# The overflow branch of an expert layer moved ahead of the first expert, and a hold on the last gate's weight splits

## The chip, the cores and the metric

The kernel runs on one core of one Trainium2 chip. The metric is the device time of one execution in microseconds, median of three runs. All times below are us unless marked ns.

## The reference

Two decoder layers over 256 tokens of width 1024, in float32. Layer 0 has a dilated attention, a dense feed-forward and a gated embedding; layer 1 has a sliding-window attention with sinks, an expert layer (the two best of 8 experts per token) and a gated embedding; a last norm ends it. The change is in the expert layer of layer 1 and in the gated product behind it:

```
logits = (h @ w_router); top_v, top_i = lax.top_k(logits, 2); wts = softmax(top_v)
gates  = einsum(one_hot(top_i, 8), wts)
for e in range(8):
    y = y + gates[..., e:e+1] * ((silu(h @ w1[e]) * (h @ w3[e])) @ w2[e])   # 1024 -> 3584 -> 1024
x = x + y
gate = sigmoid(rmsnorm(x) @ ple_w_gate);  x = x + (p @ ple_w_proj) * gate
return rmsnorm(x)
```

The weights of the 8 experts are 352 MB, 336 blocks of 1 MiB; each is read once.

## The kernel before

**Experts.** The experts are ranked by their number of tokens. Rank r has a fixed number of slots, `CAPS` (96 for the first five, 64 for the last three), and the ranks are computed in the order `TURNS = (0, 5, 1, 2, 6, 3, 4, 7)`. Rank 0 stands in the code as expert 0 itself; which expert the others are is known only at run time. Tokens that find no slot are computed by `beyond` (line 1448), a block of instructions under `tc.If(most > 0)` (line 1466); `most` is the largest overflow, read into a register of every engine by `values_load` (line 1441). In the runs here no token is left over, so the branch jumps over the block. It stands between the fourth and the fifth expert: `by_turn(TURNS[:4], ...)` (line 1438) and `by_turn(TURNS[4:], ...)` (line 1511) are two sequences, and each ends with its last sum and combine exposed. The false side of the branch holds one semaphore instruction on PE, ACT and DVE and eight on SP, one for each of the semaphores that count SP's transfers. Each waits until its semaphore has the value of everything issued so far, and then adds what the skipped block would have added.

**One expert.** `Expert` (line 1140) makes a selection matrix `P` from token positions (DVE), `gather` multiplies it with the normed tokens (32 PE products, two ACT copies to `xb`) and turns `P` into `PT`. Four chunks of the hidden width follow (1024, 1024, 1024, 512). `hidden` (line 1217) forms `H` from `w1` and `w3` in 32-column groups of PE; `hidden_tail` does silu (ACT), the product (DVE), the turning to `hT` (PE, ACT or DVE); `output` (line 1265) sums `w2` products into `Y`, one chunk behind `hidden`. After the last chunk `combine` (line 1176) copies and splits `Y` into `yh`, `yl` (ACT, DVE), spreads them back with `PT` (8 PE products) and adds to `x` (DVE). Within a sequence, gather and combine of neighbours are laid between the chunks' products.

**Routing.** `route` (line 1343) is a generator: counts of tokens by products with triangular and one matrices, `Expert` for rank 0 and its gather, then on DVE the ranking (it ends in `cnt`, ranks and overflow as integers), then the gate values (lines 1391 to 1403, DVE and one ACT exponential). `find` (line 1423) loads the seven expert numbers into registers of SP.

**Weights.** `Stream` (line 152) lists all weight blocks in order of use. SP issues them in that order, each as soon as its buffer's last reader is done; the expert layer has 17 buffers (5 `raw`, 2 `mwa`, 10 `mwb`; the `mwb` are given up after `ple_w_proj`, in the last expert's third chunk). So 17 blocks can be issued before the first expert starts. The blocks of `ple_w_gate` come last; `Stream.piece` (line 266) splits each in four pieces into a rounded part `whi` (ACT, with the norm's gain) and the rest `wlo` (DVE), in one of three buffers.

**Order.** The order on each engine's queue is fixed when the program is written, by a planner (`Flow`, line 49). It keeps a clock `now`, a time at which each engine's queue ends, and a time at which each tile is due (a block of weights 2.70 after the one before it, plus 0.95; an ACT pass over 512 columns 0.52; a split's pass on DVE 0.66; a group of four products of 512 columns 0.85). Generators are run when their time comes. The generator `Stream.ahead` (line 298) appends a piece of a split when the queues of ACT and DVE end less than `slack` (2.5 in this stage) after `now`; it is started by `next_raw` (line 253) whenever blocks to be split are loaded.

Of the kernel before, what the change touches and what calls it, by code (L numbers as in the profile page):

```python
# [15 lines left out]
OP = mybir.AluOpType  # L16
AX = mybir.AxisListType
PSUM = bass.MemoryType.PSUM

D = 1024  # L20
S = 256
NB = 2
# [6 lines left out]
NE = 8  # L29
# [122 lines left out]
class Stream:  # L152
# [3 lines left out]
    def __init__(self, nc, act, vec, flow, rawp, look, width, nraw=NRAW):  # L156
        self.nc = nc
        self.act = act
        self.vec = vec
        self.flow = flow  # L160
        self.hls = []
        self.look = look
        self.width = width
        self.phase(0)
        self.part = None
        self.specs = []
        self.loaded = 0
        self.conv = 0
        self.used = 0
        self.raw = {}  # L170
        self.ready = {}
        self.times = {}
        self.dma = 3000.0
        self.done = {}
        self.pools = []
        self.more(rawp, nraw, "raw", -1)
# [76 lines left out]
    def next_raw(self, held=0):  # L253

        i = self.used
        self.ahead_raw(i - held)
        self.load(i + 1)
        t, c, n, before, _ = self.raw.pop(i)
        self.landed(t, c * n, before)
        self.used += 1  # L260
        self.skip_raw()
        if self.conv < self.loaded:
            self.flow.start(self.ahead(self.loaded, i - held))
        return t[:, :c * n].rearrange("p (c n) -> p c n", c=c)

# [70 lines left out]
def trunk(ctx, tc, x, p, attn_norm, ffn_norm, a_w_qkv, a_w_o, kv_norm, kv_w, b_w_q, b_sinks,  # L336
# [113 lines left out]
    add_square(st, b_w_o[0])  # L450
    moe0 = len(st.specs)
    ranks = [(r,) if r else 0 for r in TURNS]
    add_moe(st, moe_seq(ranks[:4]))
    moe_cut = add_moe(st, moe_seq(ranks[4:]), 3 * len(moe_chunks) + PLE_AT, rows(ple_w_proj[1], 0, 256, 0, D))
    add_square(st, ple_w_gate[1], gcol[:, 5, :])


# [844 lines left out]
    def experts(es, nxt=None, then={}, ahead=True):  # L1302

        E = {}
        nf = len(moe_chunks)

        def begin(i):
            E[i] = es[i]()
            return E[i].gather()

        def products(i, res, f, Y):
            output(E[i], Y, res, moe_chunks[f][1], f == 0, f == nf - 1)
            if f == nf - 1:
                flow.start(E[i].combine(Y, nxt if i == len(es) - 1 else None))

        prev = None
        for i in range(len(es)):
            if i not in E:
                g = begin(i)
                if not E[i].ready:  # L1320
                    flow.spawn(g)
            Y = [psY.tile([128, 512], F32, name=f"Y{k}", tag=f"Y{k}") for k in (range(3) if E[i].ng == 3 else (0,))]
            for f, (f0, fn) in enumerate(moe_chunks):
                res = []
                g = begin(i + 1) if ahead and f == nf - 2 and i + 1 < len(es) else None
                hidden(E[i], fn, res)
                if (i, f) in then:
                    then[i, f]()
                if not ahead:
                    products(i, res, f, Y)  # L1330
                    continue
                if g is not None:
                    flow.spawn(g)
                if prev is not None:
                    products(*prev)
                prev = (i, res, f, Y)
            if not ahead:
                flow.drain()
        if ahead:
            products(*prev)  # L1340
        flow.drain()

    def route():

        while 0 not in n_f1.chosen:
            yield flow.now + 100.0
        yield flow.due(sel)
        ps = acc()
        mm(ps[:, 0:8], tri, sel[:, 0], start=True, stop=False, skip_group_check=True)
        mm(ps[:, 8:16], ones, sel[:, 0], start=False, stop=False, skip_group_check=True)  # L1350
        mm(ps[:, 16:24], ones, sel[:, 0], start=False, stop=False, skip_group_check=True)
        while 1 not in n_f1.chosen:
            yield flow.now + 100.0
        yield flow.due(sel)
        mm(ps[:, 8:16], tri, sel[:, 1], start=False, stop=False, skip_group_check=True)
        mm(ps[:, 16:24], ones, sel[:, 1], start=False, stop=True, skip_group_check=True)
        vec.scalar_tensor_tensor(posm.rearrange(g16), sel.rearrange(g16), -BIG, ps[:, 0:16], op0=OP.mult, op1=OP.add)
        if WARM2:
            warm(WARM2)
        first.append(Expert(CAPS[0], posm[:, :, 0:1], by_rank[1][:, :, 0:1]))  # L1360
        vec.tensor_copy(count, ps[:, 16:24])
        yield from first[0].gather()

        d8, a8, perm = d4[:, 0], a4[:, 0], d4[:, 1]
        vec.tensor_copy(total, count)
        vec.memset(total[:, 0:1], 2.0 * S)
        vec.tensor_tensor(d8, total[:, None, :].to_broadcast([128, NE, NE]),
                          total[:, :, None].to_broadcast([128, NE, NE]), op=OP.subtract)
        d, a = d8.rearrange(f64), a8.rearrange(f64)
        vec.scalar_tensor_tensor(a, d, 0.0, less, op0=OP.is_equal, op1=OP.mult)  # L1370
        vec.scalar_tensor_tensor(a, d, 0.0, a, op0=OP.is_gt, op1=OP.add)
        vec.tensor_reduce(rstat[:, 0:8], a8, axis=AX.X, op=OP.add)
        vec.tensor_scalar(rstat[:, 0:8], rstat[:, 0:8], -BIG, None, op0=OP.add)

        vec.tensor_tensor(perm, iota[:, 0:8][:, :, None].to_broadcast([128, NE, NE]),
                          rstat[:, None, 0:8].to_broadcast([128, NE, NE]), op=OP.is_equal)
        vec.tensor_tensor(a8, perm, iota[:, None, 0:8].to_broadcast([128, NE, NE]), op=OP.mult)
        vec.tensor_reduce(rstat[:, 0:8], a8, axis=AX.X, op=OP.add)
        vec.tensor_scalar(cnt[:, 0:8], rstat[:, 0:8], BIG, None, op0=OP.add)
        for tb in range(NB):  # L1380
            vec.tensor_tensor(a8, perm, posm[:, tb, None, :].to_broadcast([128, NE, NE]), op=OP.mult)
            vec.tensor_reduce(by_rank[0][:, tb], a8, axis=AX.X, op=OP.add)

        vec.tensor_tensor(a8, perm.rearrange("p r e -> p e r"), capt[:, None, :].to_broadcast([128, NE, NE]), op=OP.mult)
        vec.tensor_reduce(capx, a8, axis=AX.X, op=OP.add)
        vec.tensor_tensor(total, count, capx, op=OP.subtract)
        vec.tensor_reduce(rstat[:, 0:1], total, axis=AX.X, op=OP.max)
        vec.tensor_scalar(cnt[:, 8:9], rstat[:, 0:1], 0.0, None, op0=OP.max)
        ranked.append(True)
        yield flow.now + 1.0  # L1390
        for tb in range(NB):
            vec.tensor_scalar(lg[:, tb], lg[:, tb], n_f1.r[tb], None, op0=OP.mult)
        vec.tensor_reduce(rstat[:, 1:3], lg, axis=AX.X, op=OP.max)
        vec.tensor_tensor(gates, lg, rstat[:, 1:3][:, :, None].to_broadcast([128, NB, NE]), op=OP.subtract)
        act(gates, gates, AF.Exp)
        yield flow.due(gates)
        vec.tensor_tensor(gates, gates, sel, op=OP.mult)
        vec.tensor_reduce(rstat[:, 3:5], gates, axis=AX.X, op=OP.add)
        vec.reciprocal(rstat[:, 5:7], rstat[:, 3:5])
        vec.tensor_tensor(gates, gates, rstat[:, 5:7][:, :, None].to_broadcast([128, NB, NE]), op=OP.mult)  # L1400
        for tb in range(NB):
            vec.tensor_tensor(a8, perm, gates[:, tb, None, :].to_broadcast([128, NE, NE]), op=OP.mult)
            vec.tensor_reduce(by_rank[1][:, tb], a8, axis=AX.X, op=OP.add)
# [7 lines left out]
        psB = pool(f"psS{k}", 2, ps, space=PSUM)  # L1411

    first = []
    ranked = []

    def by_turn(turns, then={}, **kw):

# [4 lines left out]

    def find():

        flow.until(lambda: ranked)
        for r in TURNS:
            if r:
                which[r] = nc.values_load(cnt[0:1, r:r + 1], engines=(mybir.EngineType.SP,), min_val=0, max_val=NE - 1,
# [2 lines left out]
    st.ahead_raw(st.used)  # L1431
    moes = ExitStack()
    flow.start(route())
    flow.until(lambda: first and len(first[0].ready) == 2)
    gst.close()
    banks.close()
    expert_pools(moes, banks, 1)
    by_turn(TURNS[:4], {(0, 0): find})


    most = nc.values_load(cnt[0:1, 8:9], min_val=0, max_val=S,
                          skip_runtime_bounds_check_because="a count of at most 256 tokens")
    st.ahead_raw(st.used)
    main = st
    moes.close()
    banks.close()

    def beyond(i):

# [14 lines left out]
        selp = sel1  # L1464

    with tc.If(most > 0):
        beyond(1)
        with tc.If(most > CAP):
            beyond(2)
    ppp = pool("ppp", 1, side="right")  # L1470
    expert_pools(moes, banks, 3)


    n_p1 = Norm(div=2)
# [18 lines left out]
    def proj_p1():  # L1493
# [13 lines left out]
        st.more_split(pool("hl2", NHL), NHL)  # L1507
        xtpool = pool("xT2", 1)
        st.phase(6)

    by_turn(TURNS[4:], {(3, PLE_AT - 1): load_p1, (3, PLE_AT): proj_p1}, nxt=n_p1.half)
    st.phase(7)
    moes.close()
    banks.close()
# [87 lines left out]
```

## Time and profile before

| what | value |
|---|---|
| median of 3 runs | 1558.57 (1557.28 to 1560.46) |
| the profiled execution, its own time | 1557.69 |
| its span, first to last instruction | 1555.9 |
| PE busy | 1507.0 (97%) |
| DVE, ACT busy | 541.2 (35%), 433.9 (28%) |
| read from HBM | 452.69 MB, mean 292 GB/s |

The profiled execution lies 1.8 over its span and 0.9 under the median. PE counts as busy in almost the whole span, also where products run at half clock, so its share says little; what counts is the rate of its products in each stage, and where its rows have gaps. SP issues four blocks of the expert weights before 600, the next at 616.4 and the last at 1491.7. Lines of the profile are those of the kernel before; line 135 is the helper that records every ACT and DVE operation, so these are told apart by their tiles.

### The profile page before, as it was taken

The numbers are of one execution on the slowest core, as the hardware profiler recorded it, in microseconds if no ns is written. First come the engines' busy times: TensorE is split into PE (matmuls) and PEld (weight loads), VectorE is DVE, ScalarE is ACT, GpSimd is POOL, SyncE is SP. The second block draws the span as 40 slices with busy tenths as digits, with TensorE's granted clock in tenths as the row PEclk, the third lists the DMA queues.
The fourth block names the chain that finished last, engine by engine and source line by source line (L and its number), as shares of the span: only waits on it lengthen the run. The fifth ranks groups of instructions, "written<-read, shape, count | busy, mean of one in ns | idle before, by whom it ended". The sixth has DMA issues, their size and how long they took to land. (4 is left out here: it accounts for less than half of the span.)

```text
span 1555.9 us, 28406 instructions
## 1 busy us (share of the span) xinstructions
PE 1507.0 (97%) x11944; PEld 862.5 (55%) x11944; DVE 541.2 (35%) x1274; ACT 433.9 (28%) x851; POOL 11.3 (1%) x22
## 2 busy tenths in 40 slices
PE   7999999999999999999999999996999999999977
PEld 7999989888888887334333343332343343343325
DVE  6776767654545796200100100202001001201124
ACT  5555555554444775100000000100000010001123
POOL 0000000000000000000000000000000000000000
PEclk9999999999999999999999999997999999999998
DMA  9544445475554442999999999999799999999890
GB/s 280 154 142 143 122 122 170 136 253 186 175 204 162 136 131 78 410 403 408 409 402 408 408 402 409 409 402 382 299 402 408 409 402 409 406 405 408 353 338 28
DMA packets 214583, 455.66 MB, mean 293 GB/s; under 512 B 15440, under 2 KB 97232, under 8 KB 214448
## 3 DMA queue, kind: packets, MB, share of 16 engines
q1 hardware_dynamic: 214128, 453.31, 78.3%
q8 instruction: 95, 1.56, 0.4%
q0 software_dynamic: 176, 0.40, 0.1%
q14 instruction: 40, 0.33, 0.1%
q10 hardware_dynamic: 144, 0.07, 0.0%
HBM read 452.69 MB, written 1.05 MB: 292 GB/s over the span
## 5 line engine op out<-in xcount | busy, mean ns | idle before, releaser
L1137 PE MATMUL H<-mwb,xb 128*32 128x512 f32 (+1 forms) x3176 | 322.9, 540 | 0.2 <-DMA mwb<-in_moe_w 0.2
L135 DVE TENSOR_TENSOR wlo<-raw,whi 128x768 fp32r<-128x768 f32 (+1 forms) x180 | 188.5, 1079 | 117.8 <-ACT whi L135 117.5
L135 DVE TENSOR_TENSOR sa<-sa,H 128x512 f32<-128x512 f32 (+1 forms) x32 | 19.9, 621 | 574.6 <-PE H L1137 574.6
L1137 PEld LDWEIGHTS H<-mwb,xb 128*32 128x32 f32 x3176 | 104.9, 110 | 194.3 <-issue 169.7
L135 ACT ACTIVATE whi<-raw 128x768 fp32r<-128x768 f32 (+1 forms) x180 | 162.0, 945 | 111.0 <-PE scr L347 61.3
L135 ACT ACTIVATE sa<-H 128x512 f32<-128x512 f32 (+1 forms) x32 | 17.4, 544 | 611.0 <-PE H L1137 611.0
L1137 PE MATMUL H<-raw,xb 128*32 128x512 f32 (+1 forms) x1480 | 158.8, 546 | 0.0
L1137 PE MATMUL Y<-mwb,hT 128*32 128x512 f32 x1240 | 143.4, 594 | 0.0
L347 PE MATMUL acc<-whi,xT0h 128*128 128x384 f32 (+2 forms) x296 | 103.8, 351 | 0.0
L347 PE MATMUL acc<-wlo,xT0h 128*128 128x384 f32 (+2 forms) x296 | 101.4, 343 | 1.4 <-DVE wlo L135 1.4
L347 PE MATMUL acc<-whi,xT0l 128*128 128x384 f32 (+2 forms) x296 | 101.2, 342 | 0.1
L1137 PEld LDWEIGHTS H<-raw,xb 128*32 128x32 f32 x1480 | 49.4, 110 | 90.7 <-issue 79.7
L1137 PE MATMUL Y<-raw,hT 128*32 128x512 f32 x856 | 99.7, 593 | 0.0
L347 PE MATMUL acc<-whi,xT1h 128*128 128x384 f32 (+2 forms) x280 | 98.2, 351 | 0.3 <-ACT xT1h L135 0.3
L347 PE MATMUL acc<-whi,xT1l 128*128 128x384 f32 (+2 forms) x280 | 93.7, 335 | 0.2 <-DVE xT1l L135 0.2
L347 PE MATMUL acc<-wlo,xT1h 128*128 128x384 f32 (+2 forms) x280 | 93.4, 334 | 0.0
L1137 PEld LDWEIGHTS Y<-mwb,hT 128*32 128x32 f32 x1240 | 39.3, 110 | 83.5 <-issue 81.3
L1137 PE MATMUL H<-mwa,xb 128*32 128x512 f32 (+1 forms) x720 | 82.7, 531 | 0.0
L1137 PEld LDWEIGHTS Y<-raw,hT 128*32 128x32 f32 x856 | 27.5, 110 | 58.7 <-issue 57.0
L347 PEld LDWEIGHTS acc<-whi,xT0h 128*128 128x128 f32 x296 | 56.3, 190 | 4.6 <-issue 2.3
L347 PEld LDWEIGHTS acc<-wlo,xT0h 128*128 128x128 f32 x296 | 56.3, 190 | 4.1 <-DVE wlo L135 2.0
L347 PEld LDWEIGHTS acc<-whi,xT0l 128*128 128x128 f32 x296 | 56.1, 190 | 2.9 <-DVE xT0l L135 0.3
(222 smaller groups left out, 1867.4 us busy)
## 6 DMA issues: line engine op xcount, KB each, us to landing
mwb<-in_moe_w SPq DMA_DIRECT2D x190, 1024.0 KB, 18.3
raw<-in_moe_w SPq DMA_DIRECT2D x104, 1024.0 KB, 18.2
mwa<-in_moe_w SPq DMA_DIRECT2D x42, 1024.0 KB, 18.3
raw<-in_a_w_qkv SPq DMA_DIRECT2D x144, 256.0 KB, 4.0
raw<-in_dense_w SPq DMA_DIRECT2D x33, 1024.0 KB, 5.0
raw<-in_ple_w_gate SPq DMA_DIRECT2D x8, 1024.0 KB, 9.1
raw<-in_a_w_o SPq DMA_DIRECT2D x4, 1024.0 KB, 5.1
raw<-in_b_w_q SPq DMA_DIRECT2D x4, 1024.0 KB, 5.1
```

What stands on the lines that cost most here:

```text
L135: f(*a, **k)
L347: nc.tensor.matmul(dst, lhsT, rhs, **kw)
L1137: nc.tensor.matmul(dst, xs, w, start=start, stop=stop)
```

## The change

- The branch for tokens beyond the slots now stands ahead of the first expert. Ahead of it the routing is run to its end (`flow.drain()`), but `route` no longer computes the gate values. They are computed by `find_gates`, once inside the branch and once behind it, and `find` follows. The first expert's gather is started beside the ranking instead of ahead of it.
- All eight experts are one sequence, in the weight stream and in `by_turn`.
- `Stream.hold` stops the splits of `ple_w_gate` from being started after `ple_w_proj`, until the last chunk's turned columns (`res`) are in the queues.

```
@@ __init__ of Stream
+        self.hold = False
@@ next_raw
-        if self.conv < self.loaded:
+        if self.conv < self.loaded and not self.hold:
             self.flow.start(self.ahead(self.loaded, i - held))
@@ the list of weights
-    add_moe(st, moe_seq(ranks[:4]))
-    moe_cut = add_moe(st, moe_seq(ranks[4:]), 3 * len(moe_chunks) + PLE_AT, rows(ple_w_proj[1], 0, 256, 0, D))
+    moe_cut = add_moe(st, moe_seq(ranks), (NE - 1) * len(moe_chunks) + PLE_AT, rows(ple_w_proj[1], 0, 256, 0, D))
@@ products in experts
+            if i == len(es) - 1 and f == nf - 1:
+                flow.until(lambda: res)
+                st.hold = False
             output(E[i], Y, res, moe_chunks[f][1], f == 0, f == nf - 1)
@@ route
-        yield from first[0].gather()
+        flow.start(first[0].gather())
...
-        ranked.append(True)
-        yield flow.now + 1.0
+    def find_gates():
+        lgr, a8, perm = gates, a4[:, 0], d4[:, 1]
         for tb in range(NB):
-            vec.tensor_scalar(lg[:, tb], lg[:, tb], n_f1.r[tb], None, op0=OP.mult)
+            vec.tensor_scalar(lgr[:, tb], lg[:, tb], n_f1.r[tb], None, op0=OP.mult)
...
@@ find
-        flow.until(lambda: ranked)
@@ the expert layer
     flow.start(route())
-    flow.until(lambda: first and len(first[0].ready) == 2)
+    flow.drain()
     gst.close()
     banks.close()
-    expert_pools(moes, banks, 1)
-    by_turn(TURNS[:4], {(0, 0): find})
     most = nc.values_load(cnt[0:1, 8:9], ...)
-    st.ahead_raw(st.used)
     main = st
-    moes.close()
-    banks.close()
...
     with tc.If(most > 0):
+        find_gates()
         beyond(1)
         with tc.If(most > CAP):
             beyond(2)
     ppp = pool("ppp", 1, side="right")
-    expert_pools(moes, banks, 3)
+    expert_pools(moes, banks, 1)
+    find_gates()
+    find()
...
         st.phase(6)
+        st.hold = True
-    by_turn(TURNS[4:], {(3, PLE_AT - 1): load_p1, (3, PLE_AT): proj_p1}, nxt=n_p1.half)
+    by_turn(TURNS, {(NE - 1, PLE_AT - 1): load_p1, (NE - 1, PLE_AT): proj_p1}, nxt=n_p1.half)
```

## Rows read from the trace of the kernel before

**Rows 1.** Page, 40 slices of 38.9 us: busy tenths of PE, and GB/s.
```profile
PE   7999999999999999999999999996999999999977
...
GB/s 280 154 142 143 122 122 170 136 253 186 175 204 162 136 131 78 410 403 408 409 402 408 408 402 409 409 402 382 299 402 408 409 402 409 406 405 408 353 338 28
```

**Rows 2.** Stretches around the branch: busy (x) by engine, clock, DMA share, GB/s.
```profile
1080.00:1094.00 14.00, 7.12 (x36) 7.04 (x40) 1.56 (x5) 0.41 (x2) 1.14 (x2) 0.50 0.55 212
1094.00:1110.00 16.00, 16.00 (x134) 4.36 (x136) 0.52 (x2) 0.95 (x2) 0.00 (x0) 0.91 0.65 251
```

**Rows 3.** Timeline of PE around the branch: start, duration, operation, idle before.
```profile
1054.65 14.79 PE L1137 MATMUL Y<-mwb,hT 128*32 128x512 f32 x132
...
1086.88 7.06 PE L347 MATMUL scr<-P,xn 128*128 128x64 f32 x32 [6.89 <-DVE P L135]
1093.87 1.94 PE L1137 MATMUL H<-mwb,xb 128*32 128x512 f32 x8
```

**Rows 4.** Lines 1441 and 1466: duration in ns, first and last start.
```profile
L1441 PEldq TENSOR_LOAD <-cnt x1: 489/489/489, 1078.8 to 1078.8; - x1
...
L1466 SPq EVENT_SEMAPHORE  x8: 17/17/17, 1080.2 to 1091.1; - x8
...
L1466 SPq COMPARE_BRANCH  x1: 50/50/50, 1075.0 to 1075.0; - x1
...
L1466 PEldq COMPARE_BRANCH  x1: 6062/6062/6062, 1079.4 to 1079.4; - x1
```

**Rows 5.** Issues at 1073.1 and 1098.7: size, us from issue to landing.
```profile
mwb<-in_moe_w SPq DMA_DIRECT2D x1, 1024.0 KB, 17.9
...
mwb<-in_moe_w SPq DMA_DIRECT2D x1, 1024.0 KB, 4.9
```

**Rows 6.** Timeline of PE as the first expert starts.
```profile
627.41 3.71 PE L347 MATMUL scr<-P,xn 128*128 128x96 f32 x32
631.05 2.78 PE L1137 MATMUL H<-raw,xb 128*32 128x512 f32 x24
```

**Rows 7.** Timeline of DVE, first and last of the 20 ranking operations.
```profile
634.57 0.16 DVE L135 COPY total<-count 128x8 f32<-128x8 f32 x1
...
638.95 0.15 DVE L135 TENSOR_SCALAR cnt<-rstat 128x1 int32<-128x1 f32 x1
```

**Rows 8.** Line 1428 on SP; and the issue at 634.8, us to landing.
```profile
L1428 SPq TENSOR_LOAD <-cnt x7: 261/273/488, 652.8 to 654.9; - x7
...
raw<-in_moe_w SPq DMA_DIRECT2D x1, 1024.0 KB, 18.6
```

**Rows 9.** Issue at 1173.7, us to landing; and PE's first product from it.
```profile
mwb<-in_moe_w SPq DMA_DIRECT2D x1, 1024.0 KB, 18.8
...
1197.08 2.76 PE L1137 MATMUL H<-mwb,xb 128*32 128x512 f32 x24
```

**Rows 10.** Timeline of PE inside a sequence: half a gather, one quarter of a combine.
```profile
706.01 2.00 PE L347 MATMUL scr<-P,xn 128*128 128x64 f32 x16
...
985.03 0.50 PE L347 MATMUL scr<-yh,PT 96*128 96x512 f32 x1
...
985.69 2.78 PE L1137 MATMUL H<-raw,xb 128*32 128x512 f32 x24
```

**Rows 11.** Timeline of PE, last output of the last expert.
```profile
1506.50 3.58 PE L1137 MATMUL Y<-mwa,hT 128*32 128x512 f32 x16 [7.02 <-ACT hT L135]
1509.91 1.89 PE L1137 MATMUL Y<-raw,hT 128*32 128x512 f32 x16
```

**Rows 12.** Timelines of ACT, then of DVE, behind the last expert.
```profile
1505.45 0.72 ACT L135 ACTIVATE whi<-raw,gcol 128x512 fp32r<-128x512 f32 x1 [13.39 <-DMA raw<-in_ple_w_gate]
...
1513.26 0.58 ACT L135 ACTIVATE yh<-Y 64x512 fp32r<-64x512 f32 x1
...
1506.21 8.26 DVE L135 SCALAR_TENSOR_TENSOR wlo<-raw,gcol,whi 128x512 fp32r<-128x512 f32 x12 [13.61 <-ACT whi L135]
...
1516.44 1.41 DVE L135 SCALAR_TENSOR_TENSOR x<-scr,gater,x 128x512 f32<-128x512 f32 x2
```

More of the change, by code (lines that the diff above doesn't have):

```diff
@@ L1388, in route @@
         vec.tensor_scalar(cnt[:, 8:9], rstat[:, 0:1], 0.0, None, op0=OP.max)
-        ranked.append(True)
-        yield flow.now + 1.0
+    def find_gates():
+        lgr, a8, perm = gates, a4[:, 0], d4[:, 1]
         for tb in range(NB):
-            vec.tensor_scalar(lg[:, tb], lg[:, tb], n_f1.r[tb], None, op0=OP.mult)
-        vec.tensor_reduce(rstat[:, 1:3], lg, axis=AX.X, op=OP.max)
-        vec.tensor_tensor(gates, lg, rstat[:, 1:3][:, :, None].to_broadcast([128, NB, NE]), op=OP.subtract)
+            vec.tensor_scalar(lgr[:, tb], lg[:, tb], n_f1.r[tb], None, op0=OP.mult)
+        vec.tensor_reduce(rstat[:, 1:3], lgr, axis=AX.X, op=OP.max)
+        vec.tensor_tensor(gates, lgr, rstat[:, 1:3][:, :, None].to_broadcast([128, NB, NE]), op=OP.subtract)
         act(gates, gates, AF.Exp)
-        yield flow.due(gates)
         vec.tensor_tensor(gates, gates, sel, op=OP.mult)
@@ L1413, in trunk @@
     first = []
-    ranked = []
     def by_turn(turns, then={}, **kw):
```

## The prediction, made before the change was run

> **What bounds the kernel now.** I read the 40 slices first, then the stretches around the branch, then the timelines. From slice 17 on the expert weights come at 402 to 409 GB/s, and PE is busy in nine tenths; only slice 29 falls to 299 GB/s and PE to six, and slices 38 and 39 sag at the end [rows 1]. So inside the expert stage PE and the transfers run almost level, and the question is what each loses outside.
>
> The hole of slice 29 is the branch. PE's 132 products from 1054.65 last until 1069.4, and the next expert's first `H` product starts at 1093.87: 24.4 without weight products [rows 3]. In between lie the exposed combine, the branch, and a gather at 7.06 for 32 products. [...] The transfers have a hole too: the block issued at 1073.1 lands after 17.9, at 1091.0; the next is issued at 1098.7, when the first buffer comes free, and lands after 4.9, at 1103.6 [rows 5]. A block of 1.049 MB at 408 GB/s [rows 1] takes 2.6, so they lose 12.6 - 2.6 = 10.0.
>
> How level the two run is read by pairing blocks, in order of issue, with PE's products in order. The closest pair of the second half was issued last at 1173.7, landed 18.8 later, at 1192.5, and PE used it at 1197.1 [rows 9]: a margin of 4.6. More than that PE cannot gain on the transfers.
>
> The last hole is at the end: PE waits 7.0 for `hT` [rows 11], which stands on ACT's queue behind the first `whi`, and that one waits until 1505.45 for its block [rows 12].
>
> **The change, part by part.** Middle, PE. The 24.4 and the 1.4 go. Gather and combine come back between products at full clock: a gather is twice 2.00, a combine four times 985.69 - 985.03 = 0.66 [rows 10], together 4.0 + 2.6 = 6.6. PE gains 24.4 + 1.4 - 6.6 = 19.2.
>
> Front, PE. The gather still ends at 631.1 [rows 6]. The ranking takes 639.1 - 634.6 = 4.5 on DVE [rows 7]; it now stands beside the gather, which starts at 627.4, so the overflow count is there at 631.9. Then PE loads it into a register and branches. The load began at 1078.8, the branch at 1079.4, and it held PE's queue for 6.06 [rows 4]: 6.7 in all with the semaphore behind it. The first product starts at 631.9 + 6.7 = 638.6, against 631.05: 7.6 later. SP's jump, 1075.0 to 1080.2, took 5.2 [rows 4]; the ends are thus 6.7 and 7.6, and as it is PE that waits I take its own. PE has by then stood still for 7.5, much as the 7.0 at the end, and after those its 16 products lasted from 1506.50 to 1509.91, 3.4, where the next 16 took 1.89 with their drain [rows 11]; half clock costs 1.7. The front costs PE 7.6 + 1.7 = 9.3.
>
> [...]
>
> Front, transfers. Queued on SP behind the branch are now the settling of eight semaphores, the seven register loads of `find`, and every block from the 18th on. In the kernel before the last of the eight came at 1091.1, just when the last issued block had landed (1091.0) [rows 4, 5]: SP waits for all of its transfers. The 17th block, issued at 634.8, lands at 653.4; the register loads take 652.8 to 655.2, 2.4 [rows 8]. So the 18th block is issued at 655.9 and lands 4.9 later [rows 5], at 660.8, where an unbroken stream would have had it at 653.4 + 2.6 = 656.0. The transfers lose 4.8. PE doesn't see it: it holds 17 blocks, of which the first 16 are two chunks' `H` products at some 2.6 a block, 42 in all. If that cover were gone it would cost the 4.8.
>
> The two together. PE gains 19.2 - 9.3 = 9.9. The transfers gain 10.0 - 4.8 = 5.2 in the second half. At the closest pair the margin is 4.6 + 5.2 - 9.9 = -0.1: just met. So PE and weights both allow about 9.8, and I take 9.8. At the end of the stage slices 38 and 39 leave room below 408 GB/s [rows 1], so no further limit is reached there. Because the margin is used up, each us that SP loses more at the front costs a us.
>
> `find_gates` is some 12 DVE operations behind the branch, like the ranking's 20 in 4.5, so 2.7, and one on ACT. They lie beside the first chunk's products; uncovered they would cost 2.7. `load_p1`'s transfer, the same gathers and the order of the weights at the old cut cost nothing that PE waits for.
>
> Tail. With the hold `hT` is copied as soon as it is turned. The last two blocks of `w2` come ahead of the gate's first (there by 1505.45 [rows 12]) on the same queue, the later by 1502.9; 16 products of 1.7 behind it end near 1504.7, against 1509.91 + 1.89 = 1511.8 [rows 11]. PE is 7.1 earlier, but what is late next is `yh` and `yl` behind the splits. Before, all twelve pieces (three buffers of four) stood ahead of `yh` at 1513.26 and kept DVE for 8.26, 0.69 each, and the first `x` came at 1516.44 [rows 12]. With the planner's costs I count, from the release of the hold on: one piece before the first block's products, four more before the second's, then `yh` and `yl`; four more before the planner lets the combine go on to `x`; three behind it. So nine instead of twelve are ahead of `x` on DVE, whose queue has been full since 1506.2: 3 x 0.69 = 2.1. The ends are 0 (all twelve ahead of `x` still) and 1513.26 - 1504.8 = 8.4 (none ahead). I take 2.1, the count; the three others fall into DVE's pauses while PE turns `x`, or cost up to 0.7 each.
>
> Sum: 9.8 + 2.1 = 11.9. The profiled execution took 1557.69 for a span of 1555.9, so it would take 1545.8; the median lies 0.9 higher, so 1546.7.
>
> **The rivals.** First, slower: PE's first weight product could be held until SP is through. In the trace no weight product starts while SP settles; the first after the branch comes at 1093.87, behind 1091.1 [rows 3, 4]. Then PE starts at 655.9 instead of 638.6, 17.3 later: 1564.0. From a start at 638.6 + 11.9 = 650.5 on the change loses. Against it: the gather's products ran at 1086.88, while SP still waited, and a product waits for its own block's landing, which precedes the settling.
>
> Second, the tail gives nothing: the splits get in front of `hT` or of all of `yh`, `yl` and `x` again, that is, the hold doesn't do what it says. The time is 1546.7 + 2.1 = 1548.8. For it speaks that the order rests on a hand count.
>
> Third, the tail gives up to 8.4: 1540.4. Against it speaks that DVE's twelve passes are not removed.
>
> Fourth, the front is dearer by 2 to 7 (a longer jump under loaded transfers, a later restart on SP): 1549 to 1554. The zero margin speaks for it.
>
> [...]
>
> **How the numbers follow.** Within 0.2%, 3.1, is about what a measurement of this kernel can tell from no change: 1555.5 to 1561.7. Chances: forecast (1544.5 to 1548) 0.48; tail gives nothing 0.12; tail gives more 0.10; front dearer 0.14; cheap jump 0.02; several of these costs together, so that it ends within 0.2%, 0.08; the held first product 0.06. Faster: 0.48 + 0.12 + 0.10 + 0.14 + 0.02 = 0.86; same 0.08; slower 0.06. The range leaves out the last two and a part of the large tail, under 0.2: 1541 to 1554.5.
>
> **What would show it.** Right: the branch's rows near 632 to 639 on PE; the first `H` at 638 to 640 and its first 3 at half clock; SP's last semaphore at 653 to 654 and the next issue at 656; no slice under 390 GB/s in the middle; the fifth expert's products without a hole; `hT` copied right behind its turning, the last `Y` ending about 7 ahead of `yh`'s old place relative to the stage, five `whi` in front of `yh`. Wrong: a first `H` behind 650, PE waiting for weights for several us in the middle of the stage, or `x` still behind twelve `wlo`.

## The result, and the profile after

The changed kernel took 1551.03 (median of six runs, 1547.85 to 1551.96) where the kernel before took 1558.49 on the same chip: 7.5 less, a ratio of 0.9950 (95% interval 0.9940 to 0.9961). Forecast were 11.9 less and 1546.7. Three later series, each on another chip, ran the same two kernels again: 10.2, 9.1 and 7.9 less (ratios 0.9937, 0.9945, 0.9941). The mean of the four is 8.7, about three quarters of the forecast.

The profiled execution is the quickest of the six: 1547.85, 3.2 under the median, and its span of 1546.1 is 9.8 under that of before. Where this account subtracts one trace from the other, it explains these 9.8; the section on the experiments says where the other executions differ from this one.

The 40 slices, PE and GB/s, to be held against [rows 1]:

```profile
PE   7999999999999999799999999999999999999977
...
GB/s 281 155 144 141 126 123 157 135 267 191 163 195 186 136 110 59 359 382 403 408 406 405 409 403 408 409 402 409 409 398 409 409 393 409 408 400 408 390 357 28
```

The hole of slices 28 and 29 is gone: PE, whose six stood in slice 28, is at nine, and slice 29 has 409 GB/s instead of 299. The sag at the end of the stage is smaller (390 and 357 instead of 353 and 338). A new dent stands in slices 17 and 18, where the branch is now: PE at seven tenths in the first of them, 359 and 382 GB/s instead of 410 and 403.

The front. PE's timeline, then the branch's instructions by engine (duration in ns, first and last start) and SP's register loads, then the issues of the 17th block (634.8) and the 18th (658.0), then the stretch behind the first product (busy by engine, clock, DMA share, GB/s):

```profile
626.05 3.71 PE L348 MATMUL scr<-P,xn 128*128 128x96 f32 x32
...
637.78 11.96 PE L1137 MATMUL H<-raw,xb 128*32 128x512 f32 x96 [7.80 <-DVE gates L135]
```
```profile
L1464 SPq EVENT_SEMAPHORE  x8: 17/17/17, 644.1 to 655.7; - x8
...
L1464 PEldq COMPARE_BRANCH  x1: 6212/6212/6212, 631.2 to 631.2; - x1
...
L1464 SPq COMPARE_BRANCH  x1: 45/45/45, 638.7 to 638.7; - x1
...
L1431 SPq TENSOR_LOAD <-cnt x7: 261/268/279, 655.7 to 657.6; - x7
```
```profile
raw<-in_moe_w SPq DMA_DIRECT2D x1, 1024.0 KB, 20.8
...
raw<-in_moe_w SPq DMA_DIRECT2D x1, 1024.0 KB, 4.8
```
```profile
637.80:641.80 4.00, 4.00 (x24) 1.13 (x28) 1.93 (x11) 0.72 (x2) 1.14 (x2) 0.63 1.03 401
```

From the gather's start to the first `H` product PE took 637.78 - 626.05 = 11.73, before it was 631.05 - 627.41 = 3.64 [rows 6]: 8.1 later. (The releaser named in the row is DVE's gate values; PE's own branch held it until 631.2 + 6.2 = 637.4.) SP's last semaphore came at 655.7, when the 17th block had landed (634.8 + 20.8 = 655.6), the seven register loads took 2.3, and the 18th block went out at 658.0 and landed at 662.8. In the kernel before, the 17th landed 18.6 after the same issue time [rows 8].

The middle and the end of the stage. PE where it waited for a block in the middle, and its last two groups of the last expert:

```profile
1161.40 1.07 PE L1137 MATMUL H<-mwa,xb 128*32 128x512 f32 x8 [0.74 <-DMA mwa<-in_moe_w]
1163.96 1.50 PE L1137 MATMUL H<-mwa,xb 128*32 128x512 f32 x12 [1.49 <-DMA mwa<-in_moe_w]
```
```profile
1491.82 1.92 PE L1137 MATMUL Y<-mwa,hT 128*32 128x512 f32 x16 [0.73 <-DMA mwa<-in_moe_w]
1494.30 1.92 PE L1137 MATMUL Y<-raw,hT 128*32 128x512 f32 x16 [0.55 <-DMA raw<-in_moe_w]
```

Before, PE waited 7.02 for `hT` there [rows 11]. Now it waits for weights, and the last block of the experts is used as it lands, at 1494.3. That block's landing is the measure of the stage. In the kernel before, the last block was issued at 1491.7 and landed 11.0 later:

```profile
raw<-in_moe_w SPq DMA_DIRECT2D x1, 1024.0 KB, 11.0
```

From 1502.6 to 1494.3 is 8.4 before rounding, so the stage gained 8.4 of the 9.8, and what follows it 1.4.

The tail, ACT, DVE, and PE's first product of the gate:

```profile
1497.06 3.35 ACT L135 ACTIVATE whi<-raw,gcol 128x512 fp32r<-128x512 f32 x5 [10.87 <-DMA raw<-in_ple_w_gate]
1500.32 0.57 ACT L135 ACTIVATE yh<-Y 64x512 fp32r<-64x512 f32 x1
```
```profile
1497.82 3.40 DVE L135 SCALAR_TENSOR_TENSOR wlo<-raw,gcol,whi 128x512 fp32r<-128x512 f32 x5 [13.63 <-DMA raw<-in_ple_w_gate]
...
1503.22 2.74 DVE L135 SCALAR_TENSOR_TENSOR wlo<-raw,gcol,whi 128x512 fp32r<-128x512 f32 x4
1505.99 1.41 DVE L135 SCALAR_TENSOR_TENSOR x<-scr,gater,x 128x512 f32<-128x512 f32 x2
...
1509.38 0.74 DVE L135 SCALAR_TENSOR_TENSOR wlo<-raw,gcol,whi 128x512 fp32r<-128x512 f32 x1
```
```profile
1513.42 0.78 PE L348 MATMUL acc<-whi,xT0h 128*128 128x512 f32 x1
```

Five splits stand ahead of `yh`, four more ahead of `x`, as the prediction counted them. From the first gate block's `whi` to the first `x`: 1505.99 - 1497.06 = 8.93, before 1516.44 - 1505.45 = 10.99 [rows 12].

### The profile page after: what moved, and what is told of

It reads as the page before. It is cut to its first block, busy times and chain, and to the rows that moved or that the text cites. A ratio compares the mean times of both kernels' runs of the same rounds, so it can differ in the third digit from the quotient of the medians.

```text
span 1546.1 us, 28405 instructions
## 1 busy us (share of the span) xinstructions
PE 1500.1 (97%) x11944; PEld 858.4 (56%) x11944; DVE 541.2 (35%) x1274; ACT 435.2 (28%) x852; POOL 11.3 (1%) x22
## 4 chain that ended last, share of the span: by engine, by line
PE 53%; DMA 3%; DVE 1%; ACT 1%; issue 0%; SPq 0%; POOLq 0%; DVEq 0%; ACTq 0%
PE H L1137 32%; PE Y L1137 16%; PE scr L348 4%; DMA mwb<-in_moe_w 1%; DMA mwa<-in_moe_w 1%; PE scr L1258 1%; PE acc L348 1%; DMA raw<-in_ple_w_gate 1%; PE scr L353 0%; DVE wlo L135 0%; ACT xb L135 0%; DVE x L135 0%; DVE gate L135 0%; SPq L231 0%; DVE h L135 0%
## 5 line engine op out<-in xcount | busy, mean ns | idle before, releaser
L1137 PE MATMUL H<-mwb,xb 128*32 128x512 f32 (+1 forms) x3208 | 328.2, 539 | 0.2 <-DMA mwb<-in_moe_w 0.2
L1137 PE MATMUL Y<-mwb,hT 128*32 128x512 f32 x1192 | 138.2, 594 | 0.0
L1137 PE MATMUL H<-mwa,xb 128*32 128x512 f32 (+1 forms) x688 | 79.3, 528 | 2.2 <-DMA mwa<-in_moe_w 2.2
## 6 DMA issues: line engine op xcount, KB each, us to landing
mwb<-in_moe_w SPq DMA_DIRECT2D x190, 1024.0 KB, 18.4
```

The costliest lines, as they stand in the source:

```text
L1137: nc.tensor.matmul(dst, xs, w, start=start, stop=stop)
```

## The experiments

All edits are to the changed kernel, except where it is run as it is. Medians are of four or five runs; each series has its own control, the changed kernel run as it is, and is compared with that alone.

Four theories are set against each other. For the expert stage, W says that the stream of weights sets its end, and P that PE's late start sets it. For what follows the last `Y`, D says that the splits that stand on DVE ahead of `x` set the length, and S that the sum of all splits sets it, wherever they stand.

How far one trace can be trusted: nine of the kernels (after, the three controls, find_late, pe_late, no_branch, act_issue, find_p_late) have the same instructions behind the last `Y`. In their traces the gate's first product comes 17.2 after the end of `Y` (16.9 in find_late), but from there on they vary: the end of the span is 48.7 to 51.3 after `Y`. What varies is in the main TensorE's clock at the start of the gate's products. In the 17.2 ahead of them PE is busy for 8.7 (in after), and the clock granted in the last 12.5 of these is 0.50. The first 3.0 of the gate's products (busy by engine, clock, DMA share, GB/s), in find_late and in again3:

```profile
1513.70:1516.70 3.00, 3.00 (x15) 2.49 (x14) 1.51 (x3) 2.97 (x9) 0.56 (x1) 1.00 0.02 5
```
```profile
1515.90:1518.90 3.00, 3.00 (x9) 2.42 (x8) 1.27 (x4) 2.91 (x9) 0.56 (x1) 0.50 0.02 5
```

At a granted clock of 1.00 PE gets fifteen products into this stretch, at 0.50 nine. In order of this clock, find_late (1.00), after (0.80), again (0.63), again2 (0.56) and again3 (0.50) take 48.7, 49.9, 50.3, 50.5 and 51.1 from `Y` to the end. Why the clock comes back earlier in one execution than in another isn't known. A difference of one or two at the end, read from one pair of traces, is therefore no measure of an edit; the medians and the earlier landmarks (`x`, the gate's first product) are better ones.

| run | median | against its control |
|---|---|---|
| again, again2, again3 (controls) | 1550.25, 1549.01, 1551.59 | |
| no_hold | 1551.46 | +1.2 (again) |
| find_late | 1547.49 | -2.8 (again) |
| tail_late | 1547.04 | -3.2 (again) |
| pe_late | 1553.16 | +4.2 (again2) |
| no_branch | 1544.62 | -4.4 (again2) |
| act_issue | 1547.38 | -1.6 (again2) |
| find_p_late | 1548.57 | -3.0 (again3) |
| combo | 1545.17 | -6.4 (again3) |
| combo_later | 1543.68 | -7.9 (again3) |

**The kernel itself, three times.**

> The changed kernel itself, unaltered, beside the three that follow. Its profiled execution took 1547.85, the other five 1550.7 to 1552.0; in the profiled one the last weight block of the experts landed at 1494.3 and PE used it at once. Theory W (from the 18th block on the stream of weights sets the end of the expert stage): an execution near 1551 has its last block some 3 later, because the stream itself pauses more or longer, and PE still uses the last blocks as they land. Theory P (PE's own row of products, started 6.8 later at the front, sets it): the last block lands as before, some us ahead of its use, and PE's products have the 3 us in holes of their own. Median 1551 by both.

> The changed kernel unaltered once more, as the measure for the three that follow: 1549.5 to 1552, and in its trace the first product near 638, the 18th block of weights issued near 658 to 660, the last one used as it lands.

> The changed kernel unaltered, as the measure for the three that follow: 1549 to 1552.

The spans of the four traces are 1546.1, 1548.9, 1547.0 and 1549.8. The 17th block landed at 655.6, 657.2, 655.9 and 656.4; from the 18th to the last block the stream took 831.5, 832.2, 831.3 and 832.9; the last block was used as it landed in all four. What differs in the stream is one pause behind the 330th block (0.2, 1.3, 0.2, 1.9). From the last `Y` to the end the fastest took 49.9, the slowest 51.1. So between the extremes the 3.7 are 0.8 ahead of the 17th landing, 0.2 at the 18th block, 1.4 of stream and 1.2 of tail, the clock named above: no single cause, and PE has no hole of 3. What makes the pause come or stay away wasn't found.

**The hold alone.**

> The hold on the splits of the last gate is never set, so this is the move of the branch alone; twelve splits stand ahead of yh again, and hT behind the first of them. Theory D (the splits that stand on DVE ahead of x set the tail): the hold is worth what x came earlier against the first gate block, 10.99 - 8.93 = 2.1, less the 0.6 that the later splits gave back: 1.5 slower than the unaltered kernel, 1552.5. Rival (PE's wait of 7.0 for hT was on the path): up to 7 slower, 1558. Rival (the hold does nothing): the same, 1551.

```
         st.phase(6)
-        st.hold = True
```

```profile
1499.96 8.26 DVE L135 SCALAR_TENSOR_TENSOR wlo<-raw,gcol,whi 128x512 fp32r<-128x512 f32 x12 [14.06 <-ACT whi L135]
...
1510.20 1.41 DVE L135 SCALAR_TENSOR_TENSOR x<-scr,gater,x 128x512 f32<-128x512 f32 x2
```
```profile
1500.25 3.64 PE L1137 MATMUL Y<-mwa,hT 128*32 128x512 f32 x16 [7.01 <-ACT hT L135]
```

DVE, then PE, of no_hold: the old picture, twelve splits and PE's 7.01. It costs 1.2 in the medians, near the 1.5 expected, but the runs overlap (1550.57 to 1554.15 against 1549.51 to 1551.79), so the medians alone don't show that the hold gains anything. The traces show where it does: counted from the first gate block's `whi`, the hold brings `x` 2.07 earlier (10.99 against 8.92 in again) and the gate's first product 1.45 (17.81 against 16.36). The end comes 1.0 earlier, which is less than what equal kernels differ by there. So PE's wait of 7.0 was nearly all beside the DVE queue, as the prediction had it, and 0.6 of the 2.1 is lost again between `x` and the gate's first product. The branch's move alone is the rest of the change: 1560.48 - 1551.46 = 9.0 in that series.

**SP's register loads.**

> The seven register loads go from behind the branch to behind the first expert's first chunk, on SP behind the issues of the 18th block and those after it. SP comes from its last semaphore at 655.7 straight to the issue, so that goes out at some 655.8 instead of 658.0. Theory W: the whole stream and the end come 2.2 earlier, 1548.8. Theory P: PE's first product stays at 637.8 and nothing changes, 1551.

```
     find_gates()
-    find()
...
-    by_turn(TURNS, {(NE - 1, PLE_AT - 1): load_p1, (NE - 1, PLE_AT): proj_p1}, nxt=n_p1.half)
+    by_turn(TURNS, {(0, 0): find, (NE - 1, PLE_AT - 1): load_p1, (NE - 1, PLE_AT): proj_p1}, nxt=n_p1.half)
```

```profile
628.10 3.71 PE L348 MATMUL scr<-P,xn 128*128 128x96 f32 x32
...
639.80 10.59 PE L1137 MATMUL H<-raw,xb 128*32 128x512 f32 x84 [7.77 <-DVEq L1464]
```
```profile
L1431 SPq TENSOR_LOAD <-cnt x7: 262/268/287, 661.9 to 663.8; - x7
```

PE of find_late, then its register loads. From the gather's start to the first product it took 11.70, as in the unaltered kernel (11.73), and yet the kernel is 2.8 faster. The runs of the two don't overlap (1546.71 to 1548.66 against 1549.51 to 1551.79). The loads now stand behind the issues, and the step between the 17th and 18th landing fell from 7.3 in again to 5.3. PE's start was left as it was and the time fell all the same: theory P in its pure form falls. That a microsecond of SP's queue is just a microsecond at the end, the two traces don't show: of the 3.4 between the spans, 1.0 is the earlier landing of the 18th block (the 17th was 0.9 later in this trace), 0.8 lies between it and the last block, where the pause behind the 330th is missing that comes and goes in the unaltered kernel too, and 1.6 lie behind the last `Y`, where the two kernels are the same.

**PE later.**

> Six products of 512 columns that nobody reads are put on PE ahead of the first expert's first product; such six lasted 4.39 elsewhere in this kernel, and the part at half clock that they take over from the first weight products counts for neither side, so PE starts 4.4 later in effect. Theory W (the stream of weights sets the end of the expert stage): PE's waits for weights, 5.6 in the sum of the trace of the unaltered kernel, shrink by that, the last block lands as before, and the time moves by 0 to 0.5. Theory P (PE's late start sets it): 4.4 slower, about 1555.

```
     find()
+    t = scr()
+    for _ in range(6):
+        mm(t, n_f1.xn[0][:, :128], n_f1.xn[0][:, :512], start=True, stop=True)
```

```profile
629.60 3.71 PE L348 MATMUL scr<-P,xn 128*128 128x96 f32 x32
...
641.45 7.19 PE L348 MATMUL scr<-xn 128*128 128x512 f32 x12 [7.92 <-DVEq L1464]
648.57 1.92 PE L1137 MATMUL H<-raw,xb 128*32 128x512 f32 x16
```

PE of pe_late. The six lines make twelve products in the trace. They took 7.2, and the weight products behind them ran at full rate (16 in 1.92, as from 1491.82 on in after), so PE is later by about 7.2 - 1.5 = 5.7, not by the 4.4 aimed at. The median rises by 4.2, the means by 2.9 (1550.15 to 1554.44 against 1547.82 to 1551.20). Theory W, 0 to 0.5, falls too. PE's waits for weights shrank from 5.4 in again2 (3.8 in after, 5.9 in again; the expectation has 5.6) to 1.3, which covers most of the 5.7; but the stream itself now pauses, 0.9, 1.1 and 0.8 near the 50th block and 2.4 behind the 328th to the 330th, and takes 834.6 from the 18th to the last instead of 831.3. The account that fits is that a late PE gives its buffers up late, and that with 17 of them the stream feels it. Both limits hold at once; the split between them isn't settled closer than that.

**No branch at all.**

> The branch and the loading of its number into the registers are left out, and with them the block that would compute tokens left over; everything else stands where it was. PE's first product near 631 to 632 instead of 637.4, and no eight semaphores on SP, so the 18th block follows the 17th without the hole of 4.7. Theory W: the stage ends 4.7 earlier, 1545.5. Theory P: it ends earlier by the 6 to 7 that PE starts earlier and by the 1.5 at half clock, 1542 to 1543.

```
-    most = nc.values_load(cnt[0:1, 8:9], ...)
-    with tc.If(most > 0):
-        find_gates()
-        beyond(1)
-        with tc.If(most > CAP):
-            beyond(2)
```

```profile
626.64 3.71 PE L348 MATMUL scr<-P,xn 128*128 128x96 f32 x32
...
630.49 10.51 PE L1137 MATMUL H<-raw,xb 128*32 128x512 f32 x96
```

PE of no_branch. The branch at its new place costs 4.4. That is near W's 4.7 and not P's 7 to 8, but the number comes about in another way than W said. The stream runs from the 9th to the 18th block without any loss, where the unaltered kernel loses 4.6 (4.7 in again2) between the 17th and 18th landing and 2.3 more between the 9th and the 17th. So the front gives back 6.9 to 7.0, not 4.7. Then 4.0 go again behind the 328th block, when seven buffers are left, as 3.5 did in the kernel before, and from the 18th to the last block the stream takes 834.2 instead of 831.3. That leaves 4.1. At the last pair of blocks of the third chunk, the 321st and 322nd, PE starts 7.3 after the landing, against 3.2 in again2 and 8.1 in the kernel before, and SP issues the 329th block 18.4 after the 328th, against 14.3 and 19.2: the stream has run so far ahead that it waits for PE's buffers. Neither theory holds alone, and the match with 4.7 is in part luck.

The stretch 634 to 648 by DMA queue (packets, MB, share of 16 engines), first of the kernel before, then of after, then of no_branch:

```profile
DMA packets 1476, 5.72 MB, mean 408 GB/s; under 512 B 83, under 2 KB 83, under 8 KB 1475
...
q8 instruction: 1, 0.02, 0.5%
```
```profile
DMA packets 1461, 5.59 MB, mean 399 GB/s; under 512 B 109, under 2 KB 109, under 8 KB 1453
...
q0 software_dynamic: 96, 0.26, 5.1%
q8 instruction: 2, 0.03, 1.1%
q14 instruction: 6, 0.05, 1.0%
```
```profile
DMA packets 1488, 5.73 MB, mean 409 GB/s; under 512 B 92, under 2 KB 92, under 8 KB 1487
...
q8 instruction: 1, 0.02, 0.5%
```

With the branch, eight transfers of instructions (q8 and q14) stand among the blocks instead of one, and besides them the 0.26 MB of `p` (q0). In no_branch `p` goes out earlier, from 627.0 to 629.4, and the 7th and 8th landing lose 0.7 there, which they do in no other trace.

**Four blocks issued by ACT.**

> The 18th to the 21st block are issued by ACT, which comes out of the branch near 637 and has nothing to do until 658, instead of by SP, which waits until 655 for all its transfers and then loads seven registers. Each can go out as PE gives its buffer up, from 644.5 on every 2.6. Theory W: the hole of 4.7 in the stream is gone, the stage and the end come 4.7 earlier, 1545.5, while PE's first product stays near 637.5. Theory P: no change, 1550. If SP, out of the branch only at 658, is late for the 22nd, a part of the hole comes back there.

```
-        dma = self.nc.sync.dma_start
...
+            dma = (self.nc.scalar if self.loaded in self.on_act else self.nc.sync).dma_start
...
+    st.on_act = range(moe0 + 17, moe0 + 21)
```

```profile
L232 ACTq EVENT_SEMAPHORE  x4: 17/17/38, 656.9 to 658.4; - x4
L232 ACTq DMA_DIRECT2D raw<-in_moe_w x4: 375/424/902, 657.0 to 658.5; - x4
```

Issues on ACT of act_issue. It gains 1.6, not 4.7: ACT came out of the branch at 636.3 and then stood at its first issue until 656.9. By then the 17th block had landed (656.8) and SP's last semaphore had come (656.9); which of the two ACT waited for, the trace doesn't separate. Moving the issue to a free engine gained no more than this here, where that engine came to issue at 657.0, as late as SP's last semaphore (656.9).

**The transfers of `p`.**

> The register loads behind the first chunk as in find_late, and the two small transfers of p (0.26 MB in lines of 1 KB), which POOL starts at 638.1 in the middle of the running stream, are issued by SP behind its last semaphore instead, where the stream stands still anyway. If these transfers are what made four blocks after 638 land 2.3 later in sum, the 17th block lands 2.3 earlier against the 9th, SP spends 1.0 on issuing them, and the stream gains 1.3 over find_late's 2.2 to 2.8: 3.5 to 4.1 faster than the unaltered kernel, near 1546. If they are not, the four blocks land as late as before and SP's 1.0 is lost: 1.2 to 1.8 faster only.

```
     ppp = pool("ppp", 1, side="right")
+    p1t = ppp.tile([128, 512], F32, name="p1")
+    for tb in range(NB):
+        nc.sync.dma_start(p1t[:, 256 * tb:256 * (tb + 1)], p[1, 0, 128 * tb:128 * (tb + 1), :])
```

The register loads stand as in find_late, and the issues on POOL in `load_p1` go.

3.0 faster than its control, between the two expectations and no better than find_late in its series (2.8). From the 9th to the 17th landing the loss was 1.8 instead of find_late's 2.6, and SP's time for issuing `p` took that back (the step to the 18th lost 3.6 instead of 2.7). One pair of traces doesn't size the share of `p`: combo and combo_later below, with the same move, lose 2.3 and 2.1, and the nine traces with `p` in its place 2.2 to 3.3. The 0.7 of no_branch is the cleaner measure. What remains, 1.8 to 2.3, comes with the branch (no_branch: 0.0 at these blocks) and not with `p`. The instruction transfers are what the trace has there besides; that they are the cause is not shown, as no run took them away alone.

**The tail, a later release of the hold.**

> The hold ends behind yh and yl instead of ahead of the last products: four splits instead of nine stand on DVE ahead of the first x, and eight instead of three run beside the last product itself. Theory D: yh right behind the last Y (0.3 instead of 4.1 after it), x some 4 to 5 earlier against the last Y, and of that 3 to 5 at the end: 1546 to 1548. Rival S (the sum of all sixteen splits on DVE, 0.7 each, bounds the tail wherever they stand): PE waits inside the last product for splits instead, at most 1 gained, 1550 to 1551.

```
-            if i == len(es) - 1 and f == nf - 1:
-                flow.until(lambda: res)
-                st.hold = False
...
                 flow.start(E[i].combine(...))
+                if st.hold and i == len(es) - 1:
+                    st.hold = False
+                    flow.start(st.ahead(st.loaded, st.used))
```

> The front of find_p_late with the hold of tail_late (four splits ahead of the first x). One gain is ahead of the last block's landing and the other behind it, so they add: 3.8 + 3.2 = 7.0 faster than the unaltered kernel, near 1543. If PE has meanwhile become the limit of the stage, its waits for weights (5.0 in the trace) being used up, 1 to 2 less.

> As the run before, but the hold ends behind the last x: no split ahead of the first x, thirteen in a row beside the last product instead of eight. Theory D (what stands ahead of x on DVE sets the tail): x 2.8 earlier, 1540. Theory S (the sum of the splits sets it): PE waits for splits inside the last product, 1543 to 1544.

Combo has both edits, find_p_late and tail_late; it is 6.4 faster than its control where 7.0 were expected (3.0 and 3.2 in the two runs of one edit each, which thus add up). In combo_later the last three lines stand, with `nxt is not None` as their condition, behind the loop over the four `x` in `combine` instead. DVE of tail_late, then DVE and PE of combo_later:

```profile
1502.39 2.74 DVE L135 SCALAR_TENSOR_TENSOR wlo<-raw,gcol,whi 128x512 fp32r<-128x512 f32 x4
1505.16 1.41 DVE L135 SCALAR_TENSOR_TENSOR x<-scr,gater,x 128x512 f32<-128x512 f32 x2
```
```profile
1498.79 1.41 DVE L135 SCALAR_TENSOR_TENSOR x<-scr,gater,x 128x512 f32<-128x512 f32 x2
...
1509.61 6.71 DVE L135 SCALAR_TENSOR_TENSOR wlo<-raw,gcol,whi 128x512 fp32r<-128x512 f32 x10 [0.40 <-ACT whi L135]
```
```profile
1505.87 0.78 PE L348 MATMUL acc<-whi,xT0h 128*128 128x512 f32 x1
...
1509.63 0.50 PE L348 MATMUL acc<-whi,xT0h 128*128 128x512 f32 x1 [1.51 <-ACT whi L135]
...
1511.27 0.63 PE L348 MATMUL acc<-whi,xT0h 128*128 128x512 f32 x1
```

| from the end of the last `Y` to | again | tail_late | combo | combo_later |
|---|---|---|---|---|
| first `x` | 9.8 | 5.6 | 5.6 | 2.8 |
| gate's first product | 17.2 | 13.0 | 13.0 | 9.8 |
| end of the span | 50.3 | 45.9 | 46.5 | 47.0 |

With four splits ahead of `x` instead of nine, `x` and the gate's first product come 4.2 earlier, at the place where theory D puts it, and the tail is 4.4 shorter; the median gains 3.2, and the runs don't overlap (1545.67 to 1547.73 against 1549.51 to 1551.79). In combo_later `x` comes another 2.8 earlier and the gate's first product 3.2, but PE then waits 1.51 for the second split, and a product at 1511.27 still takes 0.63. In the three stretches of 3.0 from the gate's first product on PE is busy 2.22, 1.99 and 3.00 at a clock of 0.78, 0.79 and 0.64; in combo it is busy throughout, at 0.70, 1.00 and 1.00. From the gate's first product to the end combo_later takes 37.2, where the other traces take 31.9 to 34.0, so the gain at `x` is lost again behind it: from there on the splits limit, as theory S has it, and PE, which waits in between, has the lower clock for longer. In the two traces combo_later is quicker by 1.3 because its last `Y` ends 1.9 earlier, where the two kernels are the same. The runs of the two overlap (1543.84 to 1546.15, 1542.06 to 1544.82), so the 1.5 between their medians is not shown to come from the later release. Both beat the kernel before (ratios 0.9903, interval 0.9888 to 0.9918, and 0.9893, 0.9878 to 0.9908) and the changed one.

## Why the prediction came out as it did

The sign and the range were right, and so were the mechanisms that the sum names; the sum was 11.9 where 7.5 to 10.2 were measured, 9.8 in the profiled execution. Two terms were mis-sized: the front's loss of the transfers, with 1.4 at the end of the stage, and the tail's end, with 0.7. They make the 2.1 by which the profiled execution missed its 1545.8. The median missed its 1546.7 by 4.3; the other 2.3 of this are the choice of the execution: the profiled one lay 3.2 under its median, where 0.9 had been reckoned. Against the mean of the four series, 8.7, the sum is 3.2 too high.

**Right.** PE at the front: first product 8.1 later against the gather, forecast 7.6, with a branch of 6.21 where the row of before had 6.06 [rows 4]. Half clock: 4.0 at 0.63, with 24 products where the next 4.0, at 1.00, have 44. Counted as a part at 0.50 and the rest at 1.00, an estimate, 0.37 / 0.50 of it, 3.0, ran at half clock, which costs 1.5; the forecast had 1.7, from products of before that ran at 0.50 (1506.5 to 1509.9). SP's settling, register loads (2.3; forecast 2.4) and the hole between the 17th and 18th landing (4.6; forecast 4.8) came in the order given. The middle hole of 10.0 is gone. No run shows by itself the 1.4 that the sum adds to the 24.4 in the middle; it is an estimate from the clock there, 0.50 over 14.0 and 0.91 over the next 16.0 [rows 2], with 0.09 / 0.50 of these counted at half speed. In after the clock is 1.00 from 1070 to 1110. The margin at the closest pair was used up: five pairs ahead of it, at 1161 and 1164, PE now waits 0.74 and 1.49, and it uses that pair's second block as it lands. (In the whole stage PE waits 3.8 for weights, 2.4 of it for `H` products; several us of this in the middle had been named as a sign of being wrong, and it came in this small size.) At `x` the tail gained 2.06, forecast 2.1.

**The mis-sized term: the front's transfers.** The sum had the 17th block land at 653.4 as before, so that only the 4.8 were lost. It landed at 655.6: the blocks already under way when the engines jump lose 2.3 between the 9th and 17th landing, and so SP's last semaphore came at 655.7 instead of 653 to 654 and the next issue at 658.0 instead of 656. The prediction wrote that `p`'s transfer costs nothing that PE waits for, and gave the jump no price on the stream. Some 0.7 of it is `p` (by no_branch), which POOL had issued into the middle hole and now issues at 638, into a running stream; the rest comes with the branch. The stream's loss is thus 6.9, not 4.8, its net gain at the closest pair 1192.5 - 1189.4 = 3.1, not 5.2, and PE's 8.8 there (1197.1 to 1188.3) is the margin of 4.6 plus that, plus 1.1 because the first products of a pair need only its first block; 9.8 was forecast. At the last block it is 8.4. The prediction saw no further limit at the end of the stage, but the kernel before has pauses behind the 328th to the 330th block there (3.5, 1.2, 0.7). They stood in no term of the sum and are gone: PE starts 3.3 instead of 8.1 after the landing of the 321st and 322nd block, and gives its buffers up in time.

Why the branch takes as long as it does isn't shown. From 634 to 648 the trace has eight instruction transfers where the kernel before has one, and PE's branch, from 631.2 on, held its queue for 6.21; no run tested whether the one comes of the other.

**Mis-sized, the other term: the tail's end.** 2.1 at `x` is 1.5 to 1.7 at the gate's first product (17.81 in no_hold and 18.01 before, against 16.36), and 1.0 to 1.4 at the end (no_hold's trace 1.0, its median 1.2; the two profiled executions 50.45 - 49.04 = 1.4 from the first `whi` on), where a single trace can be off by as much, with the clock at the gate's first products. The prediction let the three splits behind `x` fall into DVE's pauses or cost up to 0.7 each and took the former; one of them (1509.38) stands ahead of the turned columns' `xT0l`, another between the two `xT0l`. That these are what cost the 0.4 to 0.6 is read from the rows; no run moved them alone.

**The executions.** The sum was made for the profiled execution and moved by the 0.9 of the kernel before; that it was 3.2 here is not explained by one cause (see the kernel itself, three times). One could think that the lost margin lets each execution's own delays show. The runs don't bear that out: in the four series those of the changed kernel spread over 4.1, 2.3, 3.4 and 3.7, those of the kernel before over 3.4, 2.6, 2.6 and 3.9.

**The rivals.** The first product held until SP is through: refuted, it ran at 637.8 and SP was through at 655.7. The tail gives nothing: refuted by no_hold at `x` (2.07) and at the gate's first product (1.45); at the end its 1.2 isn't clear of the noise. The tail gives up to 8.4: not with this release, but tail_late shows more to be there, 4.2 at `x` and 3.2 in the median. The front dearer by 2 to 7: came true with 2.3 on the stream. It had named a later restart on SP, and that is how it came, but not the cause, the blocks under way that landed late. A cheap jump, 0.02 among the chances: no, PE's branch took 6.21.

## To carry to other kernels

In this kernel, where PE and its stream of weights run level, the branch was paid on both sides. On PE it cost the jump of 6.2 and a restart at half clock (0.63 over 4.0). On the stream it stopped the issuing queue until everything issued had landed (4.6), and the blocks under way landed later (by 1.6 to 2.3 without `p`). Ask of each instruction behind it on the issuing queue whether it must stand there; with seven register loads moved behind the next issues the median was 2.8 lower. Count also what happens once the stream is ahead: without the branch it paused for 4.0 near the end, where PE hadn't given its buffers up. And work that is held back should be held until the last short chain that needs the same engine has been queued, but not past the point where its consumer starts to wait for it (PE in combo_later, 1.51 for the second split).

## What was not expected of the hardware

In every trace the stream of blocks, 2.56 apart, pauses 1.0 to 1.7 about every 104 us (after: blocks landing at 669.4, 771.2, 880.6, 982.4, 1086.6, 1195.9, 1300.0 and 1404.1). The eight pauses of the changed kernel's stage make some 11 us, more than the whole change gained.

The pauses keep step with the transfers of instructions, 16 KB each, one every 13 us. From 700 to 1400 in after there are 53 of them:

```profile
q8 instruction: 53, 0.87, 0.5%
```

Between one pause and the next there are eight, whether the pauses are close together or far apart. Two neighbouring gaps of no_branch, from 1056.8 to 1155.9 and from 1155.9 to 1270.2:

```profile
DMA packets 11392, 40.08 MB, mean 404 GB/s; under 512 B 610, under 2 KB 610, under 8 KB 11382
...
q8 instruction: 8, 0.13, 0.5%
```
```profile
DMA packets 12980, 46.20 MB, mean 404 GB/s; under 512 B 703, under 2 KB 703, under 8 KB 12970
...
q8 instruction: 8, 0.13, 0.5%
```

Over all fourteen traces, from 690 to 1450, 83 of the 85 gaps hold exactly eight such transfers, though the gaps last from 99 to 114 us. The two others lie at the branch of the kernel before (five) and behind a pause of pe_late's own (nine). A block that ends such a pause lands 2.2 to 4.6 after the start of an instruction transfer. So the pause goes with every eighth of these transfers and not with a fixed time. Why it is the eighth, and whether the transfers cause the pause, no run tested.
